# Opening of a two-layer decoder step: five conditioning pieces, another order of loads and splits, ScalarE shifting twice, constants with weight tile five

## The chip, the core and the metric

The kernel runs on one NeuronCore of one Trainium2 chip. The metric is the device time of one execution in microseconds. All arrays are float32 in device memory; the matmuls work on fp32r pairs.

## The reference

One inference step of a decoder of two layers, for 256 prompt tokens and 8 sample tokens that share all weights. Each layer is FFN, mixer, FFN, each with its own shift, scale and gate computed from a condition vector `c` (one for the prompt, eight for the samples):

```
mod  = silu(c) @ w_ada + b_ada               # 9 rows of 1024 for each layer
h    = rms_norm(x, g) * (1 + scale) + shift
FFN:   x += 0.5 * gate * (silu(h @ w1_gate) * (h @ w1_up)) @ w2
mixer: x += gate * merge(attention(h), pooling(h)) @ w_out
```

D_MODEL is 1024, the FFN is 2816 wide. The change lies in the first FFN of the first layer, ahead of it above all: there the first rows of `mod` (k = 1 is the scale, k = 0 the shift) must be known before a first normalised `h` exists.

## The kernel before

**Data.** Activations stand transposed: 128 partitions by 8 chunks of 264 columns (256 prompt, 8 sample). Every product is done as three fp32r matmuls of 264 columns on each 128x128 weight block: `whi` times `h_hi` (L492), `wlo` times `h_hi` (L493), `whi` times `h_lo` (L501, in the opening L1038). Weights come as 1 MB tiles of 16 blocks, `wraw`, into three buffers. ScalarE rounds halves of a tile to `whi` (128x1024), VectorE subtracts quarters to `wlo` (128x512).

**What sets the order.** The program writes each engine's instructions in an order of its own; a `Clock` with an estimate of each engine's time (`Engine`, L131, is the line of every VectorE and ScalarE instruction) decides when the spawned side work is written among the weight products. `Weights.get` writes casts (`high_to`), splits (`low_to`) and loads (`load_to`, L163, SP's queue) a fixed distance ahead of the product that needs them.

**Conditioning.** `w_ada` is 1024x9216 for each layer. For layer 0, k = 1 and k = 0 come first, from `ada0`, in the pieces of `FIRST`: a piece (m0, m1) covers the chunks m0 to m1 of both. `first_use` (L1014) runs 64 small matmuls for a piece and a k into the PSUM buffer `pa`; `ada_finish` transposes it on VectorE (`tt`), adds the bias (`mods`), and for the scale multiplies in the norm's gain. The other rows come as 1 MB quarters that take a `wraw` buffer in the stream of weight tiles: `ADA_AT` lists the weight tiles at which they are used. `ada_use` (L284) runs 16 matmuls for a quarter; four quarters accumulate in `pa`, which has one buffer, and with the fourth `ada_finish` is spawned 1.5 (by the planner's clock) later.

**The opening.** All of it stands in `decoder_step_kernel`, under the pool `start`. Loads go out in the order of `FIRST_LOADS`; while they fly, ScalarE and VectorE sum the squares of `x`, TensorE runs matmuls on ones (`WARM`, L1074, and `warm`, L1058), then the sum over partitions (`rms`, L415), and `rms_rows` computes the inverse root `rb` on VectorE in nine small steps and a transpose. `FIRST_ORDER` is the hand-written order of all the rest: `use` (conditioning run), `norm` (`first_norm`: VectorE makes `ht = x * scale * rb`, ScalarE `h_hi` with the shift added, VectorE `h_lo`), `split` (`whi` and `wlo` of a tile), `mm` (`first_products`: the products of a piece's chunks with a tile, two output chunks each), `warm`. Tiles 0 to 2 are worked piece by piece here, into six PSUM buffers (`mm`, `mm`, `mm`, `tr`, `sc`, `sc`); from tile 3 on the stream runs tile by tile in `ffn`, where a product pair ends in `fsi` (silu, ScalarE), `fa` (VectorE), `ah` (ScalarE) and `al` (VectorE).

The loads of small constants: `fc` (condition and identity) and `par` (biases and gains) on ScalarE's queue, `hs` (0.8 MB, needed in the mixer) on POOL's queue (L236), `cc` (mask constants) on SP's queue at weight tile 1 (L365).

## Time and profile before

| | us |
|---|---|
| median of 3 runs | 1252.69 |
| lowest to highest | 1252.32 to 1253.71 |
| the profiled execution | 1250.9 |
| its span | 1249.1 |
| TensorE busy in it | 1230.0 |
| VectorE busy | 787.7 |
| ScalarE busy | 548.5 |
| first product | 31.25 |
| first product of weight tile 3 | 52.00 |

Times on the rows are microseconds from the start of the span. A row of a timeline reads: start, length, engine, line, operation, output <- inputs, partitions x elements, how many of them; in brackets how long the engine had been idle before, and what released it. A matmul's shown length is its whole passage; the distance of two starts is what it costs.

### The profile page before, as it was taken

How to read it: one execution, taken by the hardware profiler on the slowest of the kernel's cores; microseconds unless marked ns; L12 is line 12 of the kernel's file. 1: busy time of each engine (PE TensorE's matmuls, PEld its weight loads, DVE VectorE, ACT ScalarE, POOL GpSimd, SP SyncE). 2: the span in 40 equal slices, each digit the busy share in tenths (PEclk: the TensorE clock that was granted, in tenths of full speed). 3: DMA queues.
4: the chain of work that ended last, by engine and by line, in shares of the span. 5: the costliest groups of instructions: out<-in, count | busy, mean ns of one | idle time of the engine just before them, and what ended most of it. 6: DMA issues, size and time to landing. Idle time of an engine off the chain costs nothing.

```text
span 1249.1 us, 25734 instructions
## 1 busy us (share of the span) xinstructions
PE 1230.0 (98%) x10866; PEld 1170.8 (94%) x10866; DVE 787.7 (63%) x1716; ACT 548.5 (44%) x852; POOL 4.1 (0%) x16
## 2 busy tenths in 40 slices
PE   8999999999998999999999999999999999999998
PEld 6999999989998989999989999998999998999998
DVE  4555544576887875555567555557489878655553
ACT  2344332455553544444335444344555444444431
POOL 0000000000000000000000000000000000000000
PEclk9999999999999999999999999999999999999999
DMA  9787787655365746779745778764735484887652
GB/s 391 271 304 305 306 330 270 242 197 183 112 234 217 283 172 234 262 281 368 279 160 203 257 283 299 295 248 136 272 136 198 182 327 145 341 296 272 236 181 99
DMA packets 41988, 306.26 MB, mean 245 GB/s; under 512 B 4928, under 2 KB 6208, under 8 KB 8640
## 3 DMA queue, kind: packets, MB, share of 16 engines
q1 hardware_dynamic: 41248, 303.02, 65.4%
...
q10 hardware_dynamic: 288, 0.30, 0.1%
...
## 4 chain that ended last, share of the span: by engine, by line
PE 94%; DVE 4%; issue 0%; ACT 0%; POOL 0%; DVEq 0%; ACTq 0%; POOLq 0%
PE mm L492 29%; PE mm L493 28%; PE mm L501 26%; PE pa L284 3%; PE oo L1074 1%; PE mm L514 1%; PE sc L773 1%; PE oo L813 1%; PE tr L801 1%; PE pa L1014 1%; DVE wlo L131 1%; DVE ht L131 1%; DVE h_lo L131 0%; DVE tg L131 0%; DVE o L131 0%
## 5 line engine op out<-in xcount | busy, mean ns | idle before, releaser
L131 DVE TENSOR_TENSOR wlo<-wraw,whi 128x512 fp32r<-128x512 f32 x736 | 488.9, 687 | 288.1 <-ACT whi L131 285.7
L492 PE MATMUL mm<-h_hi,whi 128*128 128x264 f32 x2088 | 597.2, 288 | 3.2 <-ACT h_hi L131 3.2
L131 ACT CAST whi<-wraw 128x1024 fp32r<-128x1024 f32 x368 | 384.8, 1049 | 473.6 <-PE mm L501 207.1
L493 PE MATMUL mm<-h_hi,wlo 128*128 128x264 f32 x2088 | 587.8, 284 | 0.3 <-DVE wlo L131 0.2
L501 PE MATMUL mm<-h_lo,whi 128*128 128x264 f32 x1952 | 552.9, 283 | 0.0
L492 PEld LDWEIGHTS mm<-h_hi,whi 128*128 128x128 f32 x2088 | 393.2, 188 | 23.0 <-issue 14.2
L493 PEld LDWEIGHTS mm<-h_hi,wlo 128*128 128x128 f32 x2088 | 393.6, 189 | 0.7 <-DVE wlo L131 0.7
L501 PEld LDWEIGHTS mm<-h_lo,whi 128*128 128x128 f32 x1952 | 366.1, 188 | 0.0
L493 PE MATMUL mm<-ah,wlo 128*128 128x264 f32 x704 | 201.1, 286 | 0.0
L501 PE MATMUL mm<-al,whi 128*128 128x264 f32 x704 | 200.2, 284 | 0.0
L492 PE MATMUL mm<-ah,whi 128*128 128x264 f32 x704 | 199.7, 284 | 0.0
L492 PEld LDWEIGHTS mm<-ah,whi 128*128 128x128 f32 x704 | 133.1, 189 | 2.5 <-issue 2.1
L493 PEld LDWEIGHTS mm<-ah,wlo 128*128 128x128 f32 x704 | 132.2, 188 | 0.0
L501 PEld LDWEIGHTS mm<-al,whi 128*128 128x128 f32 x704 | 132.1, 188 | 0.0
L131 DVE TENSOR_TENSOR fa<-fsi,mm 128x264 f32<-128x264 f32 x86 | 36.7, 427 | 69.3 <-PE mm L501 68.9
L131 DVE SCALAR_TENSOR_TENSOR x<-mm,mods,x 128x256 f32<-128x256 f32 x48 | 23.1, 482 | 39.8 <-PE mm L501 39.7
L131 ACT ACTIVATE h_hi<-ht,mods 128x256 fp32r<-128x256 f32 x48 | 20.4, 498 | 52.9 <-DVE ht L131 42.8
L131 DVE TENSOR_TENSOR al<-fa,ah 128x264 fp32r<-128x264 f32 x88 | 37.5, 427 | 0.0
L284 PE MATMUL pa<-wraw,fc 128*32 128x256 f32 x544 | 36.4, 385 | 0.0
L131 ACT CAST ah<-fa 128x264 fp32r<-128x264 f32 x88 | 35.9, 409 | 0.4 <-DVE fa L131 0.4
L131 ACT ACTIVATE fsi<-mm 128x264 f32<-128x264 f32 x87 | 33.4, 384 | 0.5 <-PE mm L1038 0.3
L492 PE MATMUL mm<-oh,whi 128*128 128x264 f32 x96 | 28.9, 301 | 0.6 <-ACT oh L131 0.6
...
## 6 DMA issues: line engine op xcount, KB each, us to landing
wraw<-in_wts_dram SPq DMA_DIRECT2D x184, 1024.0 KB, 5.5
wraw<-in_ada_dram SPq DMA_DIRECT2D x34, 1024.0 KB, 6.6
araw<-in_ada_dram SPq DMA_DIRECT2D x30, 1024.0 KB, 8.4
a<-in_ada_dram SPq DMA_DIRECT2D x2, 2048.0 KB, 14.2
a<-in_ada_dram SPq DMA_DIRECT2D x4, 1024.0 KB, 22.5
...
```

Source lines behind the costliest of these rows:

```text
L131: return f(*a, **k)
L284: nc.tensor.matmul(pa[32 * c:32 * c + 32], sc_t[:, 2 * q + r], t[:, r, c], start=(q + r == 0), stop=(q == 3 and r == 1), tile_position=(0, ...
L492: nc.tensor.matmul(ps, wh, ah, start=first, stop=False)
L493: nc.tensor.matmul(ps, wl, ah, start=False, stop=False)
L501: nc.tensor.matmul(ps, wh, al, start=False, stop=(k == n - 1))
L514: nc.tensor.matmul(ps, wh, al, start=False, stop=(k == n - 1))
L773: nc.tensor.matmul(sc[e][:, i], qn[r:r + 64, c, q0:q0 + 128], rows[r:r + 64, c, 0:nk * 128], start=True, stop=True, tile_position=(r, 0))
L801: nc.tensor.transpose(pt[:, i], sf[:, k0:k0 + 128], ident)
L813: nc.tensor.matmul(po[64 * e:64 * e + 64, g], st["vt"][:, kt, h_ * 64:h_ * 64 + 64], s[e][:, g, kt * 128:kt * 128 + 128], start=(kt == 0), ...
L1014: nc.tensor.matmul(pa[32 * c:32 * c + 32], sc_t[:, r], t[:, r, c], start=(r == 0), stop=(r == KC - 1), tile_position=(0, 32 * c))
L1074: nc.tensor.matmul(pw, wr[:, 0:P], wr[:, 0:n], start=True, stop=True)
```

## The change

1. `FIRST` has five pieces instead of three: chunks 0-1, 2-3, 4-5, 6, 7. The loads are a0 w0 a1 w1 a2 w2 a3 a4 w3.
2. `FIRST_ORDER` is rewritten: `high` and `low` stand for one half cast and one quarter split, and are put between the pieces one by one; `rms` stands after the scale run of piece 0, and the small steps of the root are mixed with those of the shift run's `ada_finish`.
3. `norm` works otherwise: `first_scale` (VectorE) makes `xr = x * rb` for a whole piece; ScalarE then writes `h_hi = xr * scale + shift` and, in a second activation, the same into `xr` itself; VectorE makes `h_lo = xr - h_hi` for a piece in one instruction. The sample columns are done by three small VectorE instructions.
4. `ADA_AT` of the first FFN: tile 2 leaves, 29 joins; all quarters move one place down the list.
5. `par` goes first on SP's queue, `cc` and `hs` are written at weight tile 5.
6. `warm` uses 512 columns; the gate chain's yields in the FFN are capped at 5.0, and the planner's clock is set to VectorE's estimate less 3.0 after the opening.

```diff
@@ -31,18 +31,20 @@
 
 
 ADA_RUNS = ((18, 6), (0, 6), (8, 6), (8, 6), (0, 6))
-ADA_AT = ((2, 4, 6, 7, 9, 10, 12, 13, 15, 16, 18, 19, 21, 22, 24, 25, 27, 28), (),
+ADA_AT = ((4, 6, 7, 9, 10, 12, 13, 15, 16, 18, 19, 21, 22, 24, 25, 27, 28, 29), (),
           (61, 63, 65, 67, 69, 71, 73, 75), (95, 98, 101, 104, 107, 110, 113, 116), ())
 
-FIRST = ((0, 4), (4, 6), (6, 8))
-FIRST_LOADS = (("a", 0), ("w", 0), ("a", 1), ("w", 1), ("w", 2), ("a", 2), ("w", 3))
-
-WARM = ((512, 14), (264, 10), (256, 10), (128, 10), (384, 8), (512, 6))
-FIRST_ORDER = (("warm", 8), ("use", 0, 1), ("use", 0, 0), ("warm", 12), ("norm", 0), ("use", 1, 1),
...
+FIRST = ((0, 2), (2, 4), (4, 6), (6, 7), (7, 8))
+FIRST_LOADS = (("a", 0), ("w", 0), ("a", 1), ("w", 1), ("a", 2), ("w", 2), ("a", 3), ("a", 4), ("w", 3))
+FIRST_ORDER = (("warm", 26), ("use", 0, 1), ("rms",), ("high", 0), ("norm", 0), ("low", 0), ("high", 1), ("low", 2),
+               ("warm", 4), ("use", 1, 1), ("mm", 0, 0), ("scale", 1), ("low", 1), ("low", 3), ("use", 1, 0),
...
 SLOPES = [2.0 ** (-8.0 * h / 12) for h in range(1, 13)]
 
 
@@ -174,6 +176,14 @@
             self.hi[i] = self.hp.tile([P, 1024], F32R, name="whi", bufs=self.bufs)
             self.A.copy(self.hi[i], self.half(i))
             self.high += 1
+
+    def low_one(self, n):
+
+        j, c = n // 2, n % 2 * 512
+        if j not in self.lo:
+            self.lo[j] = self.lp.tile([P, 1024], F32R, name="wlo", bufs=self.bufs)
+        self.V.tensor_tensor(self.lo[j][:, c:c + 512], self.half(j)[:, c:c + 512],
+                                     self.hi[j][:, c:c + 512].bitcast(F32), op=OP.subtract)
 
     def low_to(self, n):
 
@@ -229,11 +239,10 @@
     fc = cst.tile([P, F_N], F32, name="fc")
     nc.scalar.dma_start(fc, first_in)
     par = cst.tile([P, R_N], F32, name="par")
-    nc.scalar.dma_start(par, params_in)
+    nc.sync.dma_start(par, params_in)
     x = cst.tile([P, KC, NT], F32, name="x")
     cc = cst.tile([P, C_N], F32, name="cc")
     hs = cst.tile([P, 12, P], F32R, name="hs")
-    nc.gpsimd.dma_start(hs, sel_in)
 
     ident = fc[:, F_ID:F_ID + 128]
     ones_d = cst.tile([P, P], F32, name="ones_d")
@@ -361,8 +370,9 @@
             clock.spawn(ada_extra(W.slot[t + 1] - len(at_tile[t]) + n, a), 2.5)
         if u in FILL_AT and "fill" in now:
             now["fill"].load()
-        if t == 1:
+        if t == 5:
             nc.sync.dma_start(cc, consts_in)
+            nc.gpsimd.dma_start(hs, sel_in)
         if u in COPY_AT[l] and copies:
             o, i = copies.pop(0)
             nc.sync.dma_start(o, i)
@@ -551,9 +561,9 @@
             def gated(c, pg, pu, s, a):
                 A.activation(s, pg, AF.Silu)
                 V.tensor_tensor(a, s, pu, op=OP.mult)
-                yield V.done()
+                yield min(V.done(), 5.0)
                 A.copy(ah[:, c], a)
-                yield A.done()
+                yield min(A.done(), 5.0)
                 V.tensor_tensor(al[:, c], a, ah[:, c].bitcast(F32), op=OP.subtract)
 
             for c in range(FC):
@@ -1013,21 +1023,26 @@
                 for c in range(4):
                     nc.tensor.matmul(pa[32 * c:32 * c + 32], sc_t[:, r], t[:, r, c],
                                      start=(r == 0), stop=(r == KC - 1), tile_position=(0, 32 * c))
-            ada_finish(0, k, m0, m1, pa)
+            return ada_steps(0, k, m0, m1, pa)
+
+        def first_scale(j):
+
+            m0, m1 = FIRST[j]
+            V.tensor_tensor(xr[:, m0:m1], x[:, m0:m1], rb[:, 0:NT].unsqueeze(1).to_broadcast([P, m1 - m0, NT]),
+                            op=OP.mult)
 
         def first_norm(j):
             m0, m1 = FIRST[j]
-            smp = h_samples(0, 0, m0, m1)
-            next(smp)
-            smp.send((rb, hi, lo))
-            next(smp)
-            ts = [sp.tile([P, NP], F32, name="ht", bufs=4) for m in range(m0, m1)]
-            for m, t in zip(range(m0, m1), ts):
-                h_scale(0, 0, m, rb, t)
-                h_shift(0, 0, m, hi, t)
-            next(smp, None)
-            for m, t in zip(range(m0, m1), ts):
-                h_low(0, 0, m, hi, lo, t)
+            n = m1 - m0
+            for m in range(m0, m1):
+                sc, sh = mods[0][:, 1, m, 0:1], mods[0][:, 0, m, 0:1]
+                A.activation(hi[:, m, 0:NP], xr[:, m, 0:NP], AF.Identity, scale=sc, bias=sh)
+                A.activation(xr[:, m, 0:NP], xr[:, m, 0:NP], AF.Identity, scale=sc, bias=sh)
+            hs = xr[:, m0:m1, NP:NT]
+            V.tensor_tensor(hs, hs, mods[0][:, 1, m0:m1, 1:9], op=OP.mult)
+            V.tensor_tensor(hs, hs, mods[0][:, 0, m0:m1, 1:9], op=OP.add)
+            V.tensor_copy(hi[:, m0:m1, NP:NT], hs)
+            V.tensor_tensor(lo[:, m0:m1], xr[:, m0:m1], hi[:, m0:m1].bitcast(F32), op=OP.subtract)
 
         def first_products(j, *tiles):
             for t in tiles:
@@ -1037,25 +1052,35 @@
                         wh = block(ps, 16 * t + KC * e + k, hi[:, k], k == 0, False)
                         nc.tensor.matmul(ps, wh, lo[:, k], start=False, stop=(k == KC - 1))
 
-        def first_split(t):
-
-            if t != 2 or ne < 3:
-                W.high_to(2 * t + 2)
-                W.low_to(4 * t + 4)
-                return
+        def first_high(i):
+
             pools = W.hp, W.lp
-            W.hp, W.lp, W.bufs = sp, sp, 2
-            for n in (5, 6):
-                W.high_to(n)
-                W.low_to(2 * n)
+            if i // 2 == 2:
+                W.hp, W.lp, W.bufs = sp, sp, 2
+            W.high_to(i + 1)
             W.hp, W.lp, W.bufs = *pools, W.HI
 
+        def first_low(n):
+            pools = W.hp, W.lp
+            if n // 4 == 2:
+                W.hp, W.lp, W.bufs = sp, sp, 2
+            W.low_one(n)
+            W.low = n + 1
+            W.hp, W.lp, W.bufs = *pools, W.HI
+
         def warm(n):
 
-            if n:
-                pw = ps_oo.tile([P, P], F32, name="oo")
-                for _ in range(n):
-                    nc.tensor.matmul(pw, ones_d, ones_d, start=True, stop=True)
+            pw = ps_oo.tile([P, 512], F32, name="oo")
+            for _ in range(n):
+                nc.tensor.matmul(pw, wr[:, 0:P], wr, start=True, stop=True)
+
+        def first_rms():
+            vt = rms()
+            steps = first_use(0, 0)
+            rows_ = rms_rows(vt, steps)
+            for _ in steps:
+                pass
+            return rows_
 
         nc.sync.dma_start(x, xin)
...
@@ -1068,17 +1093,21 @@
                 pass
         wr = sp.tile([P, 512], F32R, name="wr")
         G.memset(wr.bitcast(F32), 1.0)
-        for n, c in WARM:
-            pw = ps_oo.tile([P, n], F32, name="oo")
-            for _ in range(c):
-                nc.tensor.matmul(pw, wr[:, 0:P], wr[:, 0:n], start=True, stop=True)
-        vt = rms()
-        rb = rms_rows(vt)
+        xr = sp.tile([P, KC, NT], F32, name="xr")
 
         V.tensor_scalar(par[:, R_G:R_PS], par[:, R_G:R_PS], 0.375, None, op0=OP.mult)
         V.tensor_scalar(qg8, par[:, R_QG:R_QG + DEPTH], 0.125, None, op0=OP.mult)
         for op, *a in FIRST_ORDER:
-            {"warm": warm, "use": first_use, "norm": first_norm, "split": first_split, "mm": first_products}[op](*a)
+            if op == "use":
+                for _ in first_use(*a):
+                    pass
+            elif op == "rms":
+                rb = first_rms()
+                first_scale(0)
+            else:
+                {"warm": warm, "norm": first_norm, "scale": first_scale, "high": first_high, "low": first_low,
+                 "mm": first_products}[op](*a)
+    clock.t = max(clock.t, V.t - 3.0)
     b, h = early, (hi, lo)
     for l in range(DEPTH):
         b, h = ffn(l, 0, b, h, (l, 1))
```

VectorE's queue ahead of the first products. Names: `tt` transposed conditioning, `rb` inverse root, `hs` and `ht` work tiles of the norm, `xr` the scaled input. Before:

```order
L131 STREAM_TRANSPOSE rb<-ny 128x288
L131 TENSOR_SCALAR par<-par 128x52
L131 TENSOR_SCALAR qg_107<-par 128x2
L131 STREAM_TRANSPOSE tt<-pa 128x128
L131 TENSOR_TENSOR mods<-tt,par 128x36
L131 SCALAR_TENSOR_TENSOR mods<-mods,par 128x36
L131 STREAM_TRANSPOSE tt<-pa 128x128
L131 TENSOR_TENSOR mods<-tt,par 128x36
L131 TENSOR_TENSOR hs<-x,mods 128x32
L131 TENSOR_TENSOR hs<-hs,rb 128x32
L131 TENSOR_TENSOR h_hi<-hs,mods 128x4x8
L131 SCALAR_TENSOR_TENSOR ht<-x,mods,rb 128x256 x4
```

and in the changed kernel:

```order
L133 SCALAR_TENSOR_TENSOR ny<-na,ny 128x9
L133 STREAM_TRANSPOSE rb<-ny 128x288
L133 TENSOR_TENSOR xr<-x,rb 128x528
L133 TENSOR_TENSOR xr<-xr,mods 128x2x8 x2
L133 CAST h_hi<-xr 128x2x8
L133 TENSOR_TENSOR h_lo<-xr,h_hi 128x528
L133 TENSOR_TENSOR wlo<-wraw,whi 128x512 x2
L133 STREAM_TRANSPOSE tt<-pa 128x64
L133 TENSOR_TENSOR mods<-tt,par 128x18
L133 SCALAR_TENSOR_TENSOR mods<-mods,par 128x18
L133 TENSOR_TENSOR xr<-x,rb 128x528
```

In place of four `ht` and four `h_lo` instructions for half of the chunks there is one `xr`, then three for the samples, then one `h_lo`; the splits of the first quarters stand directly behind it, and the next piece's transpose behind them.

TensorE's queue at the opening's start; `oo` with `wr` or `ones_d` is warm work, but `oo<-acc` is the rms sum. Before:

```order
L415 MATMUL oo<-acc,ones_d 128x288
L1058 MATMUL oo<-ones_d 128x128 x8
L1014 MATMUL pa<-a_124,fc 32x128 x32
L1014 MATMUL pa<-a_126,fc 32x128 x32
L1058 MATMUL oo<-ones_d 128x128 x12
L1014 MATMUL pa<-a_130,fc 32x64 x32
L1058 MATMUL oo<-ones_d 128x128 x3
L1014 MATMUL pa<-a_132,fc 32x64 x32
L1058 MATMUL oo<-ones_d 128x128
L492 MATMUL mm<-h_hi,whi 128x264
L493 MATMUL mm<-h_hi,wlo 128x264
L1038 MATMUL mm<-h_lo,whi 128x264
```

and changed:

```order
L1075 MATMUL oo<-wr 128x512 x26
L1024 MATMUL pa<-a_123,fc 32x64 x32
L425 MATMUL oo<-acc,ones_d 128x288
L1024 MATMUL pa<-a_125,fc 32x64 x32
L1075 MATMUL oo<-wr 128x512 x4
L1024 MATMUL pa<-a_129,fc 32x64 x32
L502 MATMUL mm<-h_hi,whi 128x264
L503 MATMUL mm<-h_hi,wlo 128x264
L1053 MATMUL mm<-h_lo,whi 128x264
```

The rms sum moved between the two runs of piece 0, and a run of piece 1 (`a_129`) stands ahead of the first product; its other run (`a_131`) and all later ones stand behind it.

VectorE's queue in the first FFN at the end of a group of four quarters (`tt<-pa 128x256` is the transpose that reads `pa`). Before, for the group that ends at weight tile 7:

```order
L131 TENSOR_TENSOR wlo<-wraw,whi 128x512 x4
L131 TENSOR_TENSOR fa<-fsi,mm 128x264
L131 TENSOR_TENSOR wlo<-wraw,whi 128x512 x3
L131 TENSOR_TENSOR al<-fa,ah 128x264
L131 TENSOR_TENSOR wlo<-wraw,whi 128x512
L131 STREAM_TRANSPOSE tt<-pa 128x256
L131 TENSOR_TENSOR mods<-tt,par 128x72
L131 TENSOR_SCALAR mods<-mods 128x72
```

and changed, for the same group, which now ends at tile 9:

```order
L133 TENSOR_TENSOR wlo<-wraw,whi 128x512 x2
L133 TENSOR_TENSOR fa<-fsi,mm 128x264
L133 TENSOR_TENSOR wlo<-wraw,whi 128x512 x2
L133 TENSOR_TENSOR al<-fa,ah 128x264
L133 TENSOR_TENSOR wlo<-wraw,whi 128x512 x2
L133 STREAM_TRANSPOSE tt<-pa 128x256
L133 TENSOR_TENSOR mods<-tt,par 128x72
L133 TENSOR_SCALAR mods<-mods 128x72
```

The transpose stands behind a split in both; in the changed kernel that split is of the weight tile whose load takes the buffer that the group's fourth quarter had, and TensorE's next run into `pa` belongs to tile 10 instead of two tiles on.

## Rows read from the trace of the kernel before

**Rows 1.** The page: busy time, share and instructions of each engine.

```profile
PE 1230.0 (98%) x10866; PEld 1170.8 (94%) x10866; DVE 787.7 (63%) x1716; ACT 548.5 (44%) x852; POOL 4.1 (0%) x16
```

**Rows 2.** Windows: stretch, length, busy PE, PEld, DVE, ACT, POOL, clock, DMA, GB/s.

```profile
20.00:31.20 11.20, 9.41 (x267) 8.28 (x260) 8.08 (x26) 3.59 (x6) 0.00 (x0) 1.00 1.01 420
31.20:52.00 20.80, 20.80 (x281) 20.34 (x280) 13.19 (x38) 8.53 (x13) 0.00 (x0) 1.00 0.65 258
52.00:250.00 198.00, 198.00 (x1762) 183.99 (x1760) 101.88 (x208) 77.39 (x111) 0.00 (x0) 1.00 0.79 293
391.90:394.50 2.60, 0.10 (x2) 0.01 (x1) 2.46 (x8) 0.00 (x0) 0.00 (x0) 1.00 0.00 0
395.70:399.20 3.50, 3.50 (x16) 3.50 (x17) 1.40 (x3) 0.82 (x1) 0.00 (x0) 0.51 0.84 274
```

**Rows 3.** Timeline of TensorE in the opening.

```profile
26.36 1.10 PE L1014 MATMUL pa<-a,fc 128*32 128x64 f32 x64
27.39 0.94 PE L1058 MATMUL oo<-ones_d 128*128 128x128 f32 x6
...
30.65 0.42 PE L1014 MATMUL pa<-a,fc 128*32 128x64 f32 x13 [1.24 <-issue]
...
31.25 0.37 PE L492 MATMUL mm<-h_hi,whi 128*128 128x264 f32 x1
...
51.88 0.28 PE L1038 MATMUL tr<-h_lo,whi 128*128 128x264 f32 x1
52.00 0.29 PE L492 MATMUL mm<-h_hi,whi 128*128 128x264 f32 x1
```

**Rows 4.** Timelines of VectorE (DVE) and ScalarE (ACT) in the opening.

```profile
18.86 0.17 DVE L131 SCALAR_TENSOR_TENSOR ny<-na,ny 128x9 f32<-128x9 f32 x1
19.07 0.48 DVE L131 STREAM_TRANSPOSE rb<-ny 128x288 f32<-128x288 f32 x1
19.47 0.15 DVE L131 TENSOR_SCALAR par<-par 128x52 f32<-128x52 f32 x1
...
28.14 0.24 DVE L131 STREAM_TRANSPOSE tt<-pa 128x64 f32<-128x64 f32 x1
28.42 0.18 DVE L131 TENSOR_TENSOR mods<-tt,par 128x18 f32<-128x18 f32 x1
...
34.41 4.91 DVE L131 TENSOR_TENSOR wlo<-wraw,whi 128x512 fp32r<-128x512 f32 x8 [0.43 <-ACT whi L131]
...
25.16 1.71 ACT L131 ACTIVATE h_hi<-ht,mods 128x256 fp32r<-128x256 f32 x4 [15.48 <-DVE ht L131]
```

**Rows 5.** Loads, size and time to landing (the first issued at 1.2); POOL's queue.

```profile
a<-in_ada_dram SPq DMA_DIRECT2D x1, 2048.0 KB, 12.0
...
1.23 0.67 POOL L236 DMA_DIRECT2D hs<-in_sel_dram  x1 [0.78 <-POOLq L1235]
...
wraw<-in_wts_dram SPq DMA_DIRECT2D x184, 1024.0 KB, 5.5
```

**Rows 6.** Timelines of PE, DVE, SP, ACT, 81 to 103; landing of the 95.73 load.

```profile
81.79 1.07 PE L284 MATMUL pa<-wraw,fc 128*32 128x256 f32 x16
94.59 1.07 PE L284 MATMUL pa<-wraw,fc 128*32 128x256 f32 x16
101.59 1.07 PE L284 MATMUL pa<-wraw,fc 128*32 128x256 f32 x16
...
85.40 0.44 DVE L131 STREAM_TRANSPOSE tt<-pa 128x256 f32<-128x256 f32 x1
...
95.73 1.69 SPq L163 DMA_DIRECT2D wraw<-in_wts_dram  x2
...
wraw<-in_wts_dram SPq DMA_DIRECT2D x1, 1024.0 KB, 5.1
...
100.91 1.05 ACT L131 CAST whi<-wraw 128x1024 fp32r<-128x1024 f32 x1 [5.59 <-DMA wraw<-in_wts_dram]
...
101.98 0.69 DVE L131 TENSOR_TENSOR wlo<-wraw,whi 128x512 fp32r<-128x512 f32 x1 [4.96 <-ACT whi L131]
```

More of the change, by code (lines that the diff above doesn't have):

```diff
@@ L33 @@
 ADA_RUNS = ((18, 6), (0, 6), (8, 6), (8, 6), (0, 6))
[L34 removed]
+ADA_AT = ((4, 6, 7, 9, 10, 12, 13, 15, 16, 18, 19, 21, 22, 24, 25, 27, 28, 29), (),
           (61, 63, 65, 67, 69, 71, 73, 75), (95, 98, 101, 104, 107, 110, 113, 116), ())
[L37 to L45 removed]
+FIRST = ((0, 2), (2, 4), (4, 6), (6, 7), (7, 8))
+FIRST_LOADS = (("a", 0), ("w", 0), ("a", 1), ("w", 1), ("a", 2), ("w", 2), ("a", 3), ("a", 4), ("w", 3))
+FIRST_ORDER = (("warm", 26), ("use", 0, 1), ("rms",), ("high", 0), ("norm", 0), ("low", 0), ("high", 1), ("low", 2),
+               ("warm", 4), ("use", 1, 1), ("mm", 0, 0), ("scale", 1), ("low", 1), ("low", 3), ("use", 1, 0),
+               ("norm", 1), ("warm", 4), ("mm", 1, 0), ("scale", 2), ("high", 2), ("low", 4), ("high", 3), ("low", 6),
+               ("mm", 0, 1), ("low", 5), ("low", 7), ("use", 2, 1), ("scale", 3), ("mm", 1, 1), ("use", 2, 0),
+               ("norm", 2), ("warm", 2), ("mm", 2, 0), ("mm", 2, 1), ("high", 4), ("low", 8), ("use", 3, 1),
+               ("high", 5), ("low", 10), ("scale", 4), ("mm", 0, 2), ("use", 3, 0), ("norm", 3), ("low", 9), ("low", 11),
+               ("mm", 1, 2), ("mm", 2, 2), ("use", 4, 1), ("mm", 3, 0), ("mm", 3, 1), ("use", 4, 0), ("norm", 4),
+               ("mm", 3, 2), ("mm", 4, 0), ("mm", 4, 1), ("mm", 4, 2), ("high", 6), ("low", 12), ("low", 13),
+               ("high", 7), ("low", 14), ("low", 15))
 SLOPES = [2.0 ** (-8.0 * h / 12) for h in range(1, 13)]
```

4 lines of the change are left out of this document (removed).

## The prediction, made blind

> **What bounds the kernel now.** I read the page first: TensorE is busy 1230.0 us of a 1249.1 us span at the full clock [rows 1], so a gain can only come from its idle stretches, and a loss is any new wait on it. Then the windows by stage: from the first product of the opening (31.25) to the first product of weight tile 3 (52.00) TensorE is busy 20.80 of 20.80, and in 52 to 250 it is busy 198.00 of 198.00 [rows 2]. So no transfer, cast or split is late there today. Before 31.25 TensorE does nothing that the result needs but the four conditioning runs and the rms sum; the rest is warm work. The time of the opening is therefore: when the first product starts, plus what TensorE still has to do, plus the waits in between. The TensorE rows of the opening [rows 3] give the durations, the VectorE and ScalarE rows [rows 4] the chains between them, and the transfer rows [rows 5] the arrivals. Last come the rows of the conditioning quarters inside FFN 1 [rows 6], which the shifted table touches.
>
> **The change part by part: when the first product can start.** Five pieces make the first loads smaller, so their data come earlier. The queues move 420 GB/s from 20 to 31.2 us, all 16 engines busy [rows 2], so arrivals go by volume. In before, the 2 MB tile of the first scale, issued at 1.2, lands 12.0 later, at 13.2 [rows 5]. Ahead of it and with it went fc (0.2 MB), x (1.1), hs (0.8) and par (0.1). In after, two 1 MB tiles stand in the place of that one, so both scale and shift of piece 0 are there at about 13.2. The hs load moves behind tile 5 in the program text, but on POOL's queue nothing stands ahead of it but three memsets and it waits for nothing, so it is issued about a microsecond later than the 1.23 of before [rows 5] and still shares the first 13 us: I cost that move at nothing (if it were truly away, 0.8 MB at 420 GB/s would bring everything 1 to 2 us earlier).
>
> From 13.2 on the start is a chain. The 64-wide conditioning run takes 1.03 to 1.10 [rows 3]: second run done at 14.9 (it queues behind the first and the rms sum). Then on VectorE a 64-wide transpose (0.28 to the next step), ten small steps at 0.21 (18.86 to 19.07), and rb (0.40 to the next): 17.7 [rows 4]. The scaling of a whole piece is 528 elements wide; the nearest row is the 512-wide split, eight in 4.91, so 0.61 to 0.71: 18.4. ScalarE then does hi and the in-place shift for two chunks, four activations at 0.41 apart [rows 4], and each shift must wait for the hi that reads the same data, which adds some 0.13 twice: 20.45. Then h_lo, 0.65: 21.1, and the first quarter split (0.69) behind it: **first block complete from 21.9** instead of 31.25. That is 9.3 us earlier.
>
> **What TensorE still has to do from there.** Products: 143 at 0.1215 (51.88 to 52.00 is one step [rows 3]) = 17.4. Conditioning runs that now stand behind the first product: three 64-wide at 1.03 = 3.1, and four 32-wide, which the trace does not show. Their bounds are half of 1.03 (columns) and 1.03 (the same number of instructions); 64 instructions in 1.03 is 16 ns each, nearer to a price per instruction than I like, so I take 0.85: 3.4 (2.1 to 4.1). Six warm matmuls of 512 columns at 0.23 (0.1215 scaled by columns) = 1.4. Sum 25.3, where before had 20.8.
>
> The Trainium skill, "TensorE: Matmul & The Clock Gate", section "Wait — 56ns, not 53.3ns?", says that starts of matmuls are never closer than about 25 ns however few columns they have; four 32-wide runs would then be an estimated 1.6 us each, 3.0 us more than I take, and the forecast 1266.5. The row of 64 matmuls in 1.03 us [rows 3] is 16 ns each and speaks against it, so it changes nothing above.
>
> **The waits in between.** Each piece has the same chain behind its last run: transpose 0.28, bias 0.21, two hi/shift pairs 1.95, h_lo 0.7, and three hand-overs of 0.06: 3.3 us, against warm work of 0.9 (piece 1) or 0.5 (piece 2) and two leading products, 0.24, in which only hi is needed. For piece 1 VectorE is also still at quarter splits when the run ends (0.5). Exposed: 3.85 - 0.93 - 0.24 = 2.7 for piece 1, 3.45 - 0.46 - 0.24 = 2.7 for piece 2. In before this chain was covered for every piece but the first by products of other tiles [rows 2]. Next: the splits of tile 2 are queued on VectorE behind the transposes of pieces 3 and 4, which wait for TensorE's run: 0.7 for quarter 10 and 1.2 for quarter 9. Piece 4 stands behind only one product group: 1.2. At the end tile 3's products wait for a ScalarE cast into space that the opening frees only with its very last product: 0.9. Sum 9.4. So tile 3 starts at 21.9 + 25.3 + 9.4 = 56.6, less 0.1 to 0.4 where such waits overlap; I take 56.4 against 52.00: **+4.4 us**. Bounds: 32-wide runs -1.3 or +0.7; arrivals 1 earlier; the 1.24 us stop with no releaser in a conditioning run [rows 3] once more, +1.2, or gone. So +2 to +7.
>
> par on the SP queue ahead of x costs x 0.4 us, hidden under the wait for the first tile until 13.2. The cc load moves from tile 1 to tile 5, one issue on SP's queue either way, and is used much later. VectorE's capped waits in the gate chain only change the order of al and wlo; TensorE has no wait from 52 to 250 to be lengthened, and the margin there (VectorE busy 102 of 198 [rows 2]) covers that: nothing.
>
> **The shifted quarters.** Each group of four quarters sums in the one PSUM buffer pa; the next group's first run may start only when VectorE's transpose tt has read the last. In before the last run of a group and the first of the next are two weight tiles apart: 81.79 and 94.59, with tt over at 85.84 [rows 6]. The new table makes them neighbours (9 and 10, 15 and 16, 21 and 22, 27 and 28), 7.00 apart as 94.59 and 101.59 are [rows 6]. And tt stands on VectorE behind the first split of a tile whose load the SP queue issues only when the group's last run frees that buffer. The same chain is in the trace behind the run at 94.59: run over at 95.66, load issued 95.73, landing 5.1 later [rows 6], cast 100.91, split 101.98 [rows 6], the next VectorE step 0.61 later (eight splits in 4.91 [rows 4]), 102.59. A tt of 0.44 there ends at 103.03; with a hand-over of 0.06 that is 1.5 after 101.59. With the page's median landing of 5.5 [rows 5] it is 1.9. I take 1.6, four times: **+6.4 us** (four times 1.0 to 2.1, +4 to +8.4). Nothing hides it: TensorE's queue is in order, and the next products stand behind pa.
>
> **Sum.** 4.4 + 6.4 = 10.8 on the profiled execution's 1250.9 gives 1261.7. The median of the runs shown is 1252.69, 1.8 above the profiled one, so I forecast 1263.5. My own range for this case: +6 to +15.4, 1258.7 to 1268.1.
>
> **The rivals.** *Clock.* The opening of after is half idle from 14 to 22 and in the waits at 26 and 36. The trace shows what an idle stretch costs: 2.5 us idle before 394.5 and a granted clock of 0.51 (the 1.2 GHz level) in 395.7 to 399.2, so 3.5 us of work done at half speed, 1.75 lost [rows 2]. Against it: the waits here are shorter and broken by work; and in before TensorE stayed at 1.00 from 20 to 31.2 while busy 9.41 of 11.20 [rows 2]. One or two such stretches make +2 to +3.5 more, 1266. The Trainium skill, same page, section "HAM oscillation — how this bites in real kernels", states that gaps in TensorE's work make the clock fall to half; the row agrees, and by that rule this rival is the likelier the longer the waits of 2.7 are.
>
> *Opening alone.* If the planner's position of tt does not bind (the load is early since SP runs ahead), the quarters cost nothing: +4.4, 1257.1. For it: in before the tt behind the run at 81.79 was over by 85.84, 3.0 behind the run's end, which neighbours would just bear [rows 6]; against it: that tt stood behind an earlier load, and the dependency of the new one on the run is hard.
>
> *Quarters alone.* Opening even: the waits come to 5 instead of 9.4, since VectorE's chains may overlap better: +6.4, 1259.1.
>
> *Faster (the other side).* The waits behind the first product vanish, because arrivals are earlier than I think and TensorE is the limit again: then tile 3 starts at 21.9 + 25.3 = 47.2, 4.8 before 52.00. With the quarters hidden as well this gives 1247.9. It decides on the two waits of 2.7 and on tt: both must be under half of what I have. For it: 9.3 us earlier start is real. Against it: each piece's chain of 3.3 is built from rows and has less than 1.2 of cover. With the quarters' waits in place the same opening gives +1.6, 1254.3, no change.
>
> **How the numbers follow.** Forecast 0.50, clock 0.08, opening alone 0.12, quarters alone 0.10, fast opening with quarters 0.08, faster 0.12. A measurement here tells about 0.2% (2.5 us) from no change. So faster 0.12, same 0.08, slower 0.80. The range leaves out the two fast-opening cases at the low end: 1255.5; at the high end it holds the forecast's own end and most of the clock case: 1269.5.
>
> **What would show it.** In the trace of after: first products at 21 to 22; TensorE waits of 2 to 3 us for h_lo twice before 40; tile 3 at 56 to 57; TensorE waits on tt of VectorE, 1.5 to 1.7 each, four times between 100 and 240, and no other wait to 250; hs issued by POOL before 3 us; 18 quarter runs as before, and the time after FFN 1 unchanged, shifted by some 11. I am wrong if tile 3 starts before 53, or if the runs behind the group ends start without a wait.

## The result, and the profile after

| | before | after |
|---|---|---|
| median | 1252.51 | 1267.45 |
| lowest to highest | 1250.85 to 1253.71 | 1264.13 to 1271.15 |
| the profiled execution | 1250.9 | 1266.1 |
| its span | 1249.1 | 1264.3 |
| first product | 31.25 | 21.33 |
| first product of weight tile 3 | 52.00 | 58.90 |

The change makes the kernel slower: ratio 1.0123, interval 1.0110 to 1.0137, some 15 us. The forecast was 1263.5, the range 1255.5 to 1269.5. TensorE is busy for as long as it was (1229.1 us against 1230.0 in [rows 1]), part of it now at half clock; the 15.2 us between the two profiled executions are waits and work at half clock. Ratios compare fast executions alone: one of e12's eleven, 1487.19 us at a granted clock of 0.75, is left out of its ratio.

The waits of TensorE in the changed kernel, over the whole span, from the view of waits. The columns are: what waited, for what, us in total, times, longest.

```profile
PE pa L1024 <- DMA a<-in_ada_dram: 6.3, 3, 3.9
PE pa L293 <- DVE tt L133: 5.5, 4, 1.9
PE tr L759 <- DVE zo L133: 5.0, 2, 2.5
PE mm L1053 <- DVE h_lo L133: 4.6, 3, 2.0
PE mm L502 <- ACT h_hi L133: 3.9, 7, 0.8
PE oo L1075 <- POOL wr L133: 1.5, 1, 1.5
PE mm L502 <- ACT fsi L133: 1.4, 2, 0.9
PE sc L503 <- DVE wlo L133: 1.3, 2, 1.1
```

The first line lies ahead of the first product. The second and the fourth did not exist before; the third did, unchanged (mixer). The windows by stage tell the rest (stretch, length, busy PE, PEld, DVE, ACT, POOL, granted clock, DMA share, GB/s):

```profile
15.50:19.40 3.90, 0.02 (x1) 0.00 (x0) 2.34 (x9) 2.86 (x5) 0.00 (x0) 0.86 1.02 426
19.40:25.10 5.70, 5.64 (x108) 5.26 (x112) 4.25 (x9) 1.42 (x2) 0.00 (x0) 0.50 1.01 420
25.10:58.90 33.80, 26.48 (x567) 22.73 (x556) 14.84 (x47) 13.10 (x20) 0.00 (x0) 1.00 0.55 216
58.90:250.00 191.10, 184.68 (x1618) 170.58 (x1619) 95.40 (x193) 72.15 (x106) 0.00 (x0) 0.99 0.78 290
233.40:236.70 3.30, 3.30 (x23) 2.03 (x24) 2.48 (x6) 0.04 (x1) 0.00 (x0) 0.50 0.19 30
```

Where [rows 2] had 20.80 of 20.80 and 198.00 of 198.00, TensorE is now idle 7.3 us between 25.1 and 58.9 and 6.4 us between 58.9 and 250. And it ran at the 1.2 GHz level (0.50) from 19.4 to 25.1, behind 3.9 us with nothing to do, and once more at 233.4, behind a wait of 1.92 for tt. At 0.50, 5.64 us of busy time is 2.8 us of slower work, and 3.3 us is 1.7. Not all of the 2.8 delays the products: some 0.8 of it lies in the conditioning run at 19.46, and the first quarter split that the products need was done only at about 21.2.

The ledger of the 15.2 us, by places: the first product of tile 3 comes 6.9 later (52.00 to 58.90); four waits on tt, 5.5; half clock behind the fourth, 1.7; one wait for fsi at 171, 0.9. Sum 15.0.

The opening in TensorE's timeline:

```profile
19.46 1.93 PE L1024 MATMUL pa<-a,fc 128*32 128x64 f32 x64 [3.94 <-DMA a<-in_ada_dram]
21.33 0.59 PE L502 MATMUL mm<-h_hi,whi 128*128 128x264 f32 x1
24.27 1.49 PE L1024 MATMUL pa<-a,fc 128*32 128x64 f32 x64
...
29.48 0.39 PE L1053 MATMUL mm<-h_lo,whi 128*128 128x264 f32 x1 [1.99 <-DVE h_lo L133]
...
39.84 0.39 PE L1053 MATMUL mm<-h_lo,whi 128*128 128x264 f32 x1 [1.99 <-DVE h_lo L133]
...
49.24 0.39 PE L503 MATMUL sc<-h_hi,wlo 128*128 128x264 f32 x1 [1.07 <-DVE wlo L133]
...
58.90 0.39 PE L502 MATMUL mm<-h_hi,whi 128*128 128x264 f32 x1 [0.55 <-ACT fsi L133]
```

The first row shows the clock in a duration: the run that took 1.10 in [rows 3] takes 1.93. The two waits of 1.99 are the chain of a piece (pieces count from 0); in ScalarE's and VectorE's timelines, for piece 1:

```profile
26.32 0.60 ACT L133 ACTIVATE h_hi<-xr,mods 128x256 fp32r<-128x256 f32 x1 [5.51 <-DVE mods L133]
26.96 0.60 ACT L133 ACTIVATE xr<-xr,mods 128x256 f32<-128x256 f32 x1
27.47 0.58 ACT L133 ACTIVATE h_hi<-xr,mods 128x256 fp32r<-128x256 f32 x1
28.09 0.60 ACT L133 ACTIVATE xr<-xr,mods 128x256 f32<-128x256 f32 x1
...
28.72 0.71 DVE L133 TENSOR_TENSOR h_lo<-xr,h_hi 128x528 fp32r<-128x528 f32 x1 [1.92 <-ACT xr L133]
```

Each of the two shifts of a chunk starts only when the hi of the same chunk is done, and VectorE's one h_lo waits for all four.

The second new wait, at the first group end (weight tiles 9 and 10), in the timelines of SP, ScalarE, VectorE and TensorE:

```profile
101.53 1.61 SPq L165 DMA_DIRECT2D wraw<-in_wts_dram  x2
...
106.46 1.05 ACT L133 CAST whi<-wraw 128x1024 fp32r<-128x1024 f32 x1 [5.38 <-DMA wraw<-in_wts_dram]
...
107.54 0.69 DVE L133 TENSOR_TENSOR wlo<-wraw,whi 128x512 fp32r<-128x512 f32 x1 [4.79 <-ACT whi L133]
108.15 0.44 DVE L133 STREAM_TRANSPOSE tt<-pa 128x256 f32<-128x256 f32 x1
...
108.64 0.64 PE L293 MATMUL pa<-wraw,fc 128*32 128x256 f32 x8 [1.17 <-DVE tt L133]
```

This is the chain of [rows 6] with tt at its end: load issued as the group's last run ends, landing under 5 us later, cast, split, tt, and only then the run.

### The profile page after: what moved, and what is told of

It is laid out like the page before. It is cut to its first block, busy times and chain, and to the rows that moved or that the text cites. A ratio compares the mean times of both kernels' runs of the same rounds, so it can differ in the third digit from the quotient of the medians.

```text
span 1264.3 us, 26118 instructions
## 1 busy us (share of the span) xinstructions
PE 1229.1 (97%) x11046; PEld 1166.9 (92%) x11046; DVE 787.5 (62%) x1720; ACT 553.0 (44%) x860; POOL 4.0 (0%) x16
## 4 chain that ended last, share of the span: by engine, by line
PE 90%; DVE 5%; DMA 3%; ACT 1%; issue 0%; SPq 0%; ACTq 0%; DVEq 0%
PE mm L502 28%; PE mm L503 27%; PE mm L511 25%; PE pa L293 3%; DMA wraw<-in_wts_dram 2%; DMA a<-in_ada_dram 1%; PE mm L524 1%; DVE wlo L133 1%; PE sc L783 1%; PE oo L823 1%; PE tr L811 1%; PE pa L1024 1%; ACT whi L133 1%; DVE h_lo L133 0%; ACT h_hi L133 0%
## 5 line engine op out<-in xcount | busy, mean ns | idle before, releaser
L502 PEld LDWEIGHTS mm<-h_hi,whi 128*128 128x128 f32 x2088 | 393.7, 189 | 26.5 <-issue 14.0
L293 PEld LDWEIGHTS pa<-wraw,fc 128*32 128x32 f32 x544 | 14.4, 110 | 16.8 <-DVE tt L133 6.4
```

What stands on the lines that cost most here:

```text
L293: nc.tensor.matmul(pa[32 * c:32 * c + 32], sc_t[:, 2 * q + r], t[:, r, c], start=(q + r == 0), stop=(q == 3 and r == 1), tile_position=(0, ...
L502: nc.tensor.matmul(ps, wh, ah, start=first, stop=False)
```

## The experiments

The first four were run together, the next four together, and the last two pairs; the kernel before had medians of 1252.59, 1252.76, 1252.8 and 1252.6 beside them. "Tile 3" is the first product of weight tile 3 in the profiled execution. The changed kernel did not run again beside them: a difference from it is one from its four executions, which lie 7 us apart.

### e1: the old quarter table in the changed kernel

```diff
-ADA_AT = ((4, 6, 7, 9, 10, 12, 13, 15, 16, 18, 19, 21, 22, 24, 25, 27, 28, 29), (),
+ADA_AT = ((2, 4, 6, 7, 9, 10, 12, 13, 15, 16, 18, 19, 21, 22, 24, 25, 27, 28), (),
```

> The changed kernel with the quarter table of before (2, 4, 6, 7, 9, ...). Theory (the group ends as neighbours make TensorE wait for tt): the four waits on tt, 1.17 + 1.21 + 1.22 + 1.92 = 5.5 us in the trace of after, are gone, and with them the stretch at half clock behind the fourth (some 1.7): 7 us less than the changed kernel, about 1260; tile 3 still starts near 58.9. Rival (the whole loss is the opening's, and the waits on tt only take up slack that another wait would take): no less than 2 us apart from the changed kernel.

Measured: 1260.91, ratio to before 1.0071 (1.0047 to 1.0096); 6.5 less than the changed kernel. Tile 3 at 58.58. No wait on tt is left, and no half clock between tile 3 and 255. Not all of the 7 us came back: waits for fsi take 1.7 here where the changed kernel has 0.9 (waits of TensorE from 60 to 255 us):

```profile
PE mm L502 <- ACT fsi L133: 1.7, 3, 0.8
```

### e2: tt one split earlier

```diff
         done = ada_use(1, ps_ada, "pa")
-        yield 1.5
+        yield 0.0
```

> The changed kernel with one number changed: the pause between a quarter's run and its transpose in the planner is 0.0 instead of 1.5, so that tt stands ahead of the split that waits for the newly loaded tile, not behind it; the table with neighbours stays. Theory (it is tt's place on VectorE, behind the split, not the neighbourhood itself): waits on tt under 0.2 each, as much gained as with the old table, 5.5 to 7 us, about 1260.5. Rival (one buffer pa with neighbours is too short in itself, wherever tt stands): at least 0.8 us at each of the four places stays, under 3 us gained.

Measured: 1261.11, ratio 1.0063 (1.0048 to 1.0078); 6.3 less than the changed kernel, though the table keeps its neighbours. From 62 to 255 us there is one wait left in the view of waits, and none on tt:

```profile
PE mm L502 <- ACT fsi L133: 0.7, 1, 0.7
```

In VectorE's timeline tt now stands ahead of the split that waits for the load:

```profile
104.59 0.44 DVE L133 STREAM_TRANSPOSE tt<-pa 128x256 f32<-128x256 f32 x1
...
109.98 0.69 DVE L133 TENSOR_TENSOR wlo<-wraw,whi 128x512 fp32r<-128x512 f32 x1 [4.45 <-ACT whi L133]
```

The gain shows although tile 3 comes 2.2 later here, at 61.11, with the opening's program unchanged: the clock is at 0.50 three times in it, from 19.9 to 23.2, 30.2 to 33.5 and 40.5 to 43.7. So the neighbours are no loss in themselves. The loss is tt's place in VectorE's queue, behind a split that waits for a load which the group's own last run releases. The rival of one buffer being too short falls.

### e3: the new table in the kernel before

```diff
-ADA_AT = ((2, 4, 6, 7, 9, 10, 12, 13, 15, 16, 18, 19, 21, 22, 24, 25, 27, 28), (),
+ADA_AT = ((4, 6, 7, 9, 10, 12, 13, 15, 16, 18, 19, 21, 22, 24, 25, 27, 28, 29), (),
```

> The kernel before with only the new quarter table. Theory: TensorE waits for tt at four places, 1.2 to 1.9 each, 5 to 7 us in all, so 1257.5 to 1259.5 with the opening unchanged (tile 3 at 52.0). Rival (the waits need the later opening or the capped gate chain of the changed kernel): within 1.5 us of before.

Measured: 1257.68, ratio 1.0039 (1.0026 to 1.0052), 5.1 more than before; tile 3 at 52.24, as before. The waits of TensorE over the span:

```profile
PE pa L284 <- DVE tt L131: 5.5, 4, 1.6
```

The table alone costs what its waits say, with the old opening and the old gate chain. The single waits are 1.12 to 1.56, and no half clock followed any of them.

### e4: warm matmuls in the idle stretch at 15.5

```diff
-("warm", 4), ("use", 1, 1)
+("warm", 20), ("use", 1, 1)
```

> The changed kernel with 20 instead of 4 warm matmuls ahead of the first run of piece 1, which fills the idle 3.94 us at 15.5 to 19.5. Theory (that idle stretch lets the clock fall to 0.5 from 18.3 to 25.1): the granted clock stays 1.0, the run of piece 1 takes 1.10 instead of 1.93, and tile 3 starts 1.5 to 2.5 earlier, since the waits for h_lo of piece 1 end earlier as well. Rival (the chain of piece 1 runs on VectorE and ScalarE and sets the time whatever the clock): tile 3 within 0.7 of 58.9, no gain.

Measured: 1268.46, ratio 1.0122 (1.0104 to 1.0139): no gain, and tile 3 at 61.00, which neither side expected. The first half of the theory held, the clock stays at 1.00 up to 33; the second did not. The first product starts 0.6 sooner, at 20.77, but TensorE then waits 0.78 for a split that it found done in the changed kernel. The windows:

```profile
15.00:33.00 18.00, 14.98 (x260) 12.40 (x258) 12.55 (x38) 8.47 (x12) 0.00 (x0) 1.00 1.01 416
33.00:41.00 8.00, 4.07 (x81) 3.02 (x81) 2.45 (x9) 3.64 (x6) 0.00 (x0) 1.00 0.92 373
41.00:44.30 3.30, 3.30 (x17) 3.30 (x16) 0.31 (x1) 0.54 (x1) 0.00 (x0) 0.50 0.04 15
```

TensorE is busy 4.07 of 8.00 from 33 to 41 (waits of 1.42, 0.52 and 1.99), and the clock falls there instead. The 1.42 is a stop inside a conditioning run for which the profile shows no releaser; the changed kernel has none there. So this execution shows that filling one gap was not enough, but not that the fall must move to the next. The profile also has a wait of 2.65 on the first tt here, against 1.17 in the changed kernel, with half clock behind it; the load behind that wait landed 6.3 after its issue, against 4.8.

### e5: the norm of before in the new order

The body of `first_norm` is that of before, `first_scale` and its steps are gone:

```diff
-            for m in range(m0, m1):
-                A.activation(hi[:, m, 0:NP], xr[:, m, 0:NP], AF.Identity, scale=sc, bias=sh)
-                A.activation(xr[:, m, 0:NP], xr[:, m, 0:NP], AF.Identity, scale=sc, bias=sh)
...
+            for m, t in zip(range(m0, m1), ts):
+                h_scale(0, 0, m, rb, t)
+                h_shift(0, 0, m, hi, t)
+            next(smp, None)
+            for m, t in zip(range(m0, m1), ts):
+                h_low(0, 0, m, hi, lo, t)
```

> The changed kernel, pieces, order and loads kept, with the norm of before: VectorE makes ht and h_lo chunk by chunk, ScalarE shifts once. Theory (the waits of TensorE for h_lo, 1.99 twice, are the chain of two pairs of activations and one h_lo for the whole piece): the third product of pieces 1 and 2 needs only the first chunk's h_lo, so each wait shrinks to 0.8 to 1.2, and tile 3 starts 2 to 3 earlier than with the doubled shift at the same clock, 1264 to 1265.5 by median. Rival (VectorE pays in ht what ScalarE saves): waits within 0.4 of 1.99, tile 3 unmoved.

Measured: 1264.43, ratio 1.0090 (1.0075 to 1.0105), 3.0 less than the changed kernel. TensorE no longer waits for h_lo; it waits for h_hi, which comes 0.8 later behind the run than in the changed kernel, since ht must be made first (TensorE, the only two waits at pieces 1 and 2):

```profile
27.47 0.39 PE L502 MATMUL mm<-h_hi,whi 128*128 128x264 f32 x1 [0.90 <-ACT h_hi L133]
37.11 0.39 PE L502 MATMUL mm<-h_hi,whi 128*128 128x264 f32 x1 [1.36 <-ACT h_hi L133]
```

Each piece's stop shrinks from 0.0 + 1.99 to 0.90, and from 0.56 + 1.99 to 1.36. Yet tile 3 stands at 58.69, hardly moved, since this execution has half clock in 17.3 to 24.1 and again in 37.8 to 41.1. The two intervals do not meet, so the doubled shift costs something; the profile cannot say how much of the 3.0 is the chain's and how much is the clock's.

### e6: another order only

```diff
...
-               ("mm", 0, 1), ("low", 5), ("low", 7), ("use", 2, 1), ("scale", 3), ("mm", 1, 1), ("use", 2, 0),
-               ("norm", 2), ("warm", 2), ("mm", 2, 0), ("mm", 2, 1), ("high", 4), ("low", 8), ("use", 3, 1),
-               ("high", 5), ("low", 10), ("scale", 4), ("mm", 0, 2), ("use", 3, 0), ("norm", 3), ("low", 9), ("low", 11),
-               ("mm", 1, 2), ("mm", 2, 2), ("use", 4, 1), ("mm", 3, 0), ("mm", 3, 1), ("use", 4, 0), ("norm", 4),
...
+               ("use", 2, 1), ("use", 2, 0), ("low", 5), ("low", 7), ("norm", 2), ("mm", 0, 1), ("mm", 1, 1),
+               ("mm", 2, 0), ("mm", 2, 1), ("scale", 3), ("high", 4), ("low", 8), ("high", 5), ("low", 10),
+               ("use", 3, 1), ("use", 3, 0), ("low", 9), ("norm", 3), ("mm", 0, 2), ("mm", 1, 2), ("low", 11),
+               ("mm", 3, 0), ("mm", 3, 1), ("scale", 4), ("use", 4, 1), ("use", 4, 0), ("norm", 4), ("mm", 2, 2),
...
```

> The changed kernel with another FIRST_ORDER and nothing else: the products of tile 1 (pieces 0 and 1) stand behind the runs of piece 2, those of tile 2 behind the runs of piece 3, so that TensorE has 2.9 us of products while a piece's h_lo is made. Theory (the opening loses by uncovered chains, 9.4 us of waits by the sum of the prediction): the wait of 0.56 + 1.99 before piece 2's products and the 1.07 and 0.26 for splits go; tile 3 starts at 53 to 55 instead of 58.9, by median 1262 to 1264. Rival (arrivals or total work hold TensorE, not the order): tile 3 within 1.5 of 58.9.

Measured: 1261.23, ratio 1.0060 (1.0043 to 1.0077), 6.2 less than the changed kernel and with nothing but the order changed; tile 3 at 54.12, 4.8 earlier. Of the 4.8 an estimated 1.1 is the clock's, which is at 0.50 only from 20.2 to 23.6 here (3.4 us of work against 5.64). The waits of TensorE from 20 to 62 us:

```profile
PE mm L502 <- ACT h_hi L133: 1.3, 1, 1.3
PE mm L1053 <- DVE h_lo L133: 1.2, 2, 0.9
PE pa L1024 <- issue: 1.2, 1, 1.2
PE pa L1024 <- DVE tt L133: 1.0, 3, 0.4
PE mm L502 <- ACT fsi L133: 0.6, 1, 0.6
```

The wait of 0.56 + 1.99 at piece 2 is down to 0.36, and those for splits are gone. The rival, arrivals or total work, falls. The four waits on tt in the FFN stayed, 6.7 in all in this profile, so most of what is left to the kernel before lies there and not in the opening.

### e7: hs late in fact

```diff
+            G.tensor_copy(hs[:, 0, 0:1], mods[0][:, 0, KC - 1, 0:1])
             nc.gpsimd.dma_start(hs, sel_in)
```

> The changed kernel with hs truly late: a copy of one column from the last shift row stands ahead of its load on POOL's queue, so that the load is issued only near 52. Theory (the move in the program text moves nothing, since POOL waits for nothing): arrivals of pieces 0 and 1 come 1 to 2 us earlier than in the changed kernel, first products about 1 earlier, tile 3 0.5 to 1.5 earlier. Rival (the queue's order by itself decides, and hs only takes idle engine time): arrivals within 0.4.

Measured: 1266.23, ratio 1.0103 (1.0085 to 1.0120). POOL's queue, and the landing of the first 1 MB tile of conditioning, here and, in the second block, in the changed kernel, where both loads are under way at once:

```profile
52.28 0.18 POOL L133 CAST hs<-mods 128x1 fp32r<-128x1 f32 x1 [50.83 <-DVE mods L133]
52.77 0.67 POOL L376 DMA_DIRECT2D hs<-in_sel_dram  x1 [0.31 <-POOL hs L133]
...
a<-in_ada_dram SPq DMA_DIRECT2D x1, 1024.0 KB, 7.1
```

```profile
1.40 0.67 POOL L375 DMA_DIRECT2D hs<-in_sel_dram  x1
...
a<-in_ada_dram SPq DMA_DIRECT2D x1, 1024.0 KB, 9.1
```

The tile lands 2.0 sooner, the first product is at 19.62 (1.7 sooner), tile 3 at 56.77 (2.1 sooner). So the move of hs in the program text moved nothing on the chip: it is issued at 1.40, 0.17 later than in [rows 5]. The median moved by only 1.2, and the two intervals overlap, so by time it cannot be told from the changed kernel: this execution has a wait of 3.45 on the fourth tt and half clock from 230.7 to 237.5.

### e8, e10: all together

e8 has the pieces and loads of the change, the order of e6, the norm of e5, the table of e1, hs as in e7 and the warm work of e4. e10 is e8 with this order:

```diff
-FIRST_ORDER = (("warm", 26), ("use", 0, 1), ("rms",), ("high", 0), ("norm", 0), ("low", 0), ("high", 1), ("low", 2),
-               ("warm", 20), ("use", 1, 1), ("mm", 0, 0), ("use", 1, 0), ("low", 1), ("low", 3),
-               ("norm", 1), ("warm", 4), ("mm", 1, 0), ("high", 2), ("low", 4), ("high", 3), ("low", 6),
-               ("use", 2, 1), ("use", 2, 0), ("low", 5), ("low", 7), ("norm", 2), ("mm", 0, 1), ("mm", 1, 1),
+FIRST_ORDER = (("warm", 32), ("use", 0, 1), ("rms",), ("high", 0), ("norm", 0), ("low", 0), ("high", 1), ("low", 2),
+               ("warm", 14), ("use", 1, 1), ("mm", 0, 0), ("use", 1, 0), ("norm", 1), ("low", 1), ("low", 3),
+               ("use", 2, 1), ("mm", 1, 0), ("high", 2), ("low", 4), ("high", 3), ("low", 6),
+               ("use", 2, 0), ("norm", 2), ("low", 5), ("low", 7), ("mm", 0, 1), ("mm", 1, 1), ("mm", 2, 0),
...
```

> All of it together: the five pieces and loads of the changed kernel, the order of e6, the norm of before, the quarter table of before, hs late, 20 warm matmuls ahead of piece 1's first run. Theory: start of the first products at 20 to 21, waits of 3 us in all instead of 9.4, the clock at 1.00 through most of the opening, tile 3 at 49 to 52, no wait on tt: 1250 to 1253, level with or a little under before. Rival (five pieces cost more than they bring in any order): tile 3 not before 54, 1255 or more.

> As e8, with the splits that piece 2 needs moved behind the norm of piece 1 (they stand ahead of it on VectorE in e8, 25.4 to 26.6), the first run of pieces 2, 3 and 4 put between product groups so that two runs never follow each other in pa, 32 opening warm matmuls and 14 instead of 20 later. Theory: the wait of 2.11 for h_hi of piece 1 shrinks under 1, the waits of 0.37, 0.31, 0.31 on tt go, the clock stays at 1.00 in the opening, tile 3 at 49.5 to 51.5 instead of 53.3: 1248.5 to 1250.5. Rival (the clock or the arrival of piece 4 holds it): tile 3 not before 52.5, no less than e8.

Measured: e8 1251.98, ratio 0.9991 (0.9982 to 1.0000), tile 3 at 53.26. e10 1250.54, ratio 0.9985 (0.9976 to 0.9994), tile 3 at 49.61, the clock at 1.00 through the opening. e8 is short of its 49 to 52 by a first product at 22.18, behind half clock from 13.3 to 16.9, and by a wait of 2.1 (TensorE, 20 to 62 us), which e10 removes:

```profile
PE mm L503 <- ACT h_hi L133: 2.1, 1, 2.1
```

In e10, from 15 to 56 us, the longest wait is for the arrival of piece 2:

```profile
PE pa L1025 <- DMA a<-in_ada_dram: 2.8, 1, 2.8
PE pa L1025 <- issue: 1.0, 1, 1.0
PE mm L503 <- ACT fsi L133: 0.6, 1, 0.6
```

So with five pieces tile 3 can come 2.4 us sooner than before. That is not the pieces' gain alone: hs late brings 1.55 of it in the kernel before (e9), which leaves some 0.8 for pieces, order and warm work together, and by time e10 and e9 overlap. That five pieces cost more than they bring in any order is refuted as far as being level with before goes; that they gain by themselves is not shown, and no run has them alone. Of the 2.4, 1.7 is given back behind tile 3 to waits for fsi.

### e9: hs late in the kernel before

```diff
-    nc.gpsimd.dma_start(hs, sel_in)
...
+            G.tensor_copy(hs[:, 0, 0:1], mods[0][:, 0, KC - 1, 0:1])
+            nc.gpsimd.dma_start(hs, sel_in)
```

> The kernel before with only hs truly late (behind a copy that waits for the last shift row). Theory (arrivals set the first product of before, since its second 1 MB tile of scale lands at 18.1 and the chain behind it ends at 31.25): arrivals 1.9 earlier (0.79 MB at 420 GB/s), first product at 29.4 to 30, tile 3 1.2 to 1.9 earlier, 1250.8 to 1251.4. Rival (the chain of piece 1's runs and splits sets it, not arrivals): within 0.5 of before.

Measured: 1251.36, ratio 0.9993 (0.9984 to 1.0001). First product at 29.68 and tile 3 at 50.45, 1.55 earlier, as the theory has it; by time it cannot be told from before. (The tile that lands at 18.1 in before is one of 2 MB.) In the profiled execution the half clock in the second layer's mixer lasts twice as long as in before (1001.4 to 1008.2), which takes 1.7 back. Whether that follows from the change or is chance, one profile cannot say.

### e11, e12: the planner edits

```diff
-                yield min(V.done(), 5.0)
+                yield V.done()
...
-                yield min(A.done(), 5.0)
+                yield A.done()
...
-    clock.t = max(clock.t, V.t - 3.0)
```

e11 is e10 with all three lines changed so, e12 with the first two, the cap.

> e10 without the two planner edits of the change: the gate chain's yields without the cap of 5.0, and without the line that sets the planner's clock after the opening. Theory (the prediction's own: they change only the order of al, ah and wlo, no product waits for it): time within 1.0 of e10, 1249.5 to 1251.5, and the waits for fsi in the first FFN (1.35 at 102, 0.32 at 61 in e10) stay. Rival (the edits place fsi behind a cast that waits for a load, which before did not do): those waits go, 1.5 to 2 us gained, 1248.5 to 1249.

> e10 without the cap of 5.0 alone; the line on the planner's clock stays. Theory: as e11, within 1.0 of e10. Rival (the cap is what moves fsi): the waits for fsi go here as in e11; if they go there and stay here, it is the clock line.

Measured: e11 1249.55, ratio 0.9978 (0.9970 to 0.9987); e12 1250.47, ratio 0.9985 (0.9976 to 0.9995). The waits for fsi from 56 to 255 us in e10, then from 15 to 255 in e12 and in e11 (these two hold the 0.6 at tile 3 too):

```profile
PE mm L503 <- ACT fsi L133: 1.7, 2, 1.3
```

```profile
PE mm L503 <- ACT fsi L133: 1.2, 2, 0.6
```

```profile
PE mm L503 <- ACT fsi L133: 0.8, 2, 0.6
```

Behind tile 3 they are 1.7 in e10, 0.64 in e12 (at 61.3) and 0.22 in e11 (at 100.4). So the cap seems to take part of it and the clock line another; the rival is nearer the truth than my "nothing". The times of the three overlap, so that rests on the waits of one profile each. The opening is the same program in all three, and its clock is not: at 1.00 in e10 behind a wait of 2.82, at 0.50 from 26.5 to 29.6 in e11 behind 3.17 and from 25.5 to 28.7 in e12 behind 3.66. e11 is the fastest kernel of this study, 0.22% (0.13 to 0.30%) under before, some 2.8 us.

## Why the prediction came out as it did

**Direction, range and the two places: right.** Tile 3 came 6.9 later (forecast 4.4), and the waits on tt took 5.5 (forecast 6.4). e6 and e2 show both causes: another order alone brings 4.8 of the 6.9 back, and tt one place earlier all of the 5.5. What the sum does not have is the clock, and the 0.9 for fsi.

**Start of the first product: right.** Forecast 21.9 for the first complete block; the first product starts at 21.33. The claim that hs is not moved is shown by its issue at 1.40 and by e7.

**Waits in the opening: size nearly right.** Forecast 9.4 in six places; all six are there (2.0 and 2.55 for the chains, 0.26 and 1.07 for quarters, 0.82 at piece 4, 0.55 at tile 3, 7.2 as idle time). Idle time is counted from the modelled end of the matmul before, so the gap from start to start is longer: 2.27 where 1.99 is shown, and some 8.4 in all above the usual step of 0.12. e6 shows that it is cover that lacks. The chain of piece 2 went into the sum with 3.45 although its terms give 3.3, an error of 0.15. The activations were taken at 0.41 apart; they start 0.51 and 0.63 apart. A 32-wide run took 0.70 from start to start (its length is 0.76) where I had 0.85 with bounds of about 0.5 and 1.03. By the floor of about 25 ns from start to start in the Trainium skill, "TensorE: Matmul & The Clock Gate", section "Wait — 56ns, not 53.3ns?", it would have been an estimated 1.6; this row too speaks against it here.

**Clock: the step that failed.** The forecast had tile 3 at 56.4 and put a fallen clock beside it as a rival with 0.08. It fell: 0.50 from 19.4 to 25.1, behind 3.9 us of idle, and again at 233.4, which costs 1.7. Of the 2.8 in the opening about 2.0 delays the products; tile 3 is 2.5 late of the forecast. Together they are most of the 4.4 by which the profiled execution (1266.1 against 1261.7) passes the forecast. The rest nearly cancels, and that is luck: the first product came 0.6 sooner and the four short runs took 0.6 less, while the first product behind each run or wait takes 0.22 or 0.23 to the next start instead of 0.12, thirteen times, some 1.4 that the sum lacks.

What led me wrong were two arguments. "The waits here are shorter" than the 2.5 of [rows 2] was false: one is 3.94. And before, which keeps 1.00 while busy 9.41 of 11.20, has no stop above 1.24 in that stretch; the new order left one of 3.94. The rival named the stage, half idle from 14 to 22 (it is busy 4.06 of 8.00), but the sum took no loss for it. The Trainium skill, page "TensorE: Matmul & The Clock Gate", section "HAM oscillation — how this bites in real kernels", states that gaps make the clock fall; the trace agrees with 0.50 behind 3.9 us idle. e4 adds that filling one gap was not enough.

One profile is not the median. The four executions of the changed kernel, 1264.13, 1266.1, 1268.8 and 1271.15, have mean granted clocks of 0.996, 0.993, 0.989 and 0.989; the kernel before, beside the experiments, has 0.995 to 0.997. From these an estimated 4 to 7 of the 15 us are the clock's, and the spread of the changed kernel, 7.0, is of the size that 0.007 of the clock gives over 1264 us (8.9).

**Quarters: right.** Forecast four waits of 1.6, 6.4 in all; measured 1.17, 1.21, 1.22 and 1.92, 5.5 in all; alone in e3, 5.1 by the median. e2 shows the cause, tt's place behind the split. The rivals that took them as hidden fall. The size of each wait follows the landing of the load behind it, as the forecast's chain has it. Issue to landing, of the load behind the first wait of the changed kernel (1.17) and behind the fourth of e7 (3.45):

```profile
wraw<-in_wts_dram SPq DMA_DIRECT2D x1, 1024.0 KB, 4.8
```

```profile
wraw<-in_wts_dram SPq DMA_DIRECT2D x1, 1024.0 KB, 6.9
```

In e3 landings of 4.8, 5.0, 5.1 and 5.2 go with waits of 1.12, 1.38, 1.48 and 1.56; the changed kernel's fourth has 5.3 and 1.92.

**Planner edits: too small.** "Nothing" was about 0.9 in the changed kernel's profile, if the wait for fsi there has the same cause, which no run tested in that kernel, and up to 1.5 in e10 against e11. "No other wait to 250" was wrong by it. The view of margins (VectorE busy 102 of 198) was the wrong view for a question of order: a short instruction behind a cast that waits for a load is late however idle the engine is. In e10 fsi stands at 101.68 behind a cast that began at 100.73, when its load had come, and TensorE waits 1.35 for it.

**Not settled.** Why the same load lands 4.8 after its issue in one place or execution and 6.9 in another; why a wait of 2.71 on tt in e5 left the clock at 1.00 and 1.92 in the changed kernel did not; how the loss of the opening divides between pieces, order and doubled shift, since no run has the five pieces alone.
